# A two-layer streaming encoder on one core: another order of columns for TensorE's operands

## The chip, the core and the metric

The kernel runs on one core of one Trainium2 chip. The metric is the device time of one execution in microseconds (us), the median of repeated runs. One further execution was recorded by the hardware profiler; its trace is what the views below are taken from. The engines are called as the profile calls them: PE is TensorE's matmul, PEld its weight load, DVE is VectorE, ACT is ScalarE, POOL is GpSimd, SP is SyncE, which issues most of the DMAs.

## The reference

The reference is one inference step of a two-layer encoder with model width 2048. Layer 0 mixes frames by a gated MLP (gMLP), layer 1 by multi-scale retention with 8 heads; after each comes a dense SwiGLU layer with a hidden width of 5632, and after each of the four a LayerNorm of the residual sum. 256 frames of a new stream and 32 frames of a running one go through the same weights.

```python
def swiglu(x, w_in, w_out):
    gate, up = jnp.split(x @ w_in, 2, axis=-1)
    return (jax.nn.silu(gate) * up) @ w_out

def trunk(x, ...):
    for i in range(DEPTH):                       # 2
        if i % 2 == 0:
            h, v = gmlp_mix(x, w_a_in[j], ..., w_a_out[j])
        else:
            h, s = retention_mix(x, pos, states[j], w_b_in[j], w_b_out[j])
        x = layer_norm(ALPHA * x + h, ...)
        x = layer_norm(ALPHA * x + swiglu(x, w_ffn_in[i], w_ffn_out[i]), ...)
```

All data are float32. What costs the work are eight dense products: `a_in` (2048 to 4096), `a_out` (2048 to 2048), `b_in` (2048 to 12288), `b_out` (4096 to 2048), and for each of two layers `f_in` (2048 to 11264) and `f_out` (5632 to 2048), each for 288 frames.

## The kernel before

**Layout of the work.** Activations lie transposed: a channel of 128 in the partitions, the 288 frames (256 of the prompt, 32 of the running stream) along the free axis. Weights are the stationary operand in blocks of 128 x 128, the activations the moving operand with 288 columns, and an output tile of 128 channels x 288 frames gathers in one PSUM bank over all blocks of the contraction.

**Precision in three matmuls.** Each float32 value is split in a high part (rounded to the type fp32r) and a low part (what is left). `Core.step` therefore issues three fp32r matmuls for a block (lines 104 to 106): high weights by high activations, high weights by low activations, low weights by high activations. Every matmul of the program comes with its own weight load in the trace.

**Weights.** They come from HBM in the order of use, in chunks of 8 blocks: 128 partitions x 1024 values, 512 KB (`wpack`). `Core.prep` loads a chunk into one of three tiles `raw` (SP's queue, line 73) and splits it into `whi` (a copy on ACT, line 420) and `wlo` (a subtraction on DVE, line 421), of which there are four tiles each. It is called three chunks ahead. `Core.blk` (line 81) hands out block j of a chunk: in the kernel before, 128 adjacent columns. The order in which blocks are used is written down while the program is built, and the host packs `wpack` by it, outside the measured time.

**Order of the work.** The order on PE is the order of the program text. `Core.tiles` and `Core.group` run over output tiles; `evac` functions read a finished bank on ACT or DVE; `Core.after` puts small jobs (norms, transposes through DRAM, retention scores) a few output tiles later. The four accumulating banks rotate.

**Moving tiles.** `moving` (line 413) makes tiles whose rows are 320 values (1280 bytes) long and whose data begin 4 values (16 bytes) into a row. They hold the activations for `a_in`, `b_in`, `f_in` (`xh`, `xl`), `a_out` (`g_sh`, `g_sl`), `f_out` (`hh`, `hl`) and `b_out` (`r_oh`, `r_ol`). Just behind a LayerNorm the kernel starts the next product before the norm is known: `PostNorm.start` runs 12 output tiles with 290 columns, the 288 frames and two columns for gain and bias, and corrects the result afterwards. All other dense matmuls have 288 columns.

**Where the tiles lie.** Within a partition the program's layout puts 8,320 bytes of scratch and constants first, then eleven weight tiles of 4096 bytes (three `raw`, four `whi`, four `wlo`), which thus begin at 128 modulo 256, up to byte 53,376. Then comes the placeholder tile `shift` of line 900, 128 bytes that nothing uses, and `xh` at 53,504. All rows of moving tiles are multiples of 256 bytes apart, so the data of all of them begin at 16 modulo 256.

Of the kernel before, what the change touches and what calls it, by code (L numbers as in the profile page):

```python
# [10 lines left out]
F32 = mybir.dt.float32  # L11
# [8 lines left out]
P = 128  # L20
# [4 lines left out]
NT = NP + NS  # L25
# [13 lines left out]
CB = 8  # L39
# [7 lines left out]
class Core:  # L47
# [33 lines left out]
    def blk(self, w, k, m):  # L81
        i = len(self.order)
        self.order.append((w, k, m))
        c, j = divmod(i, CB)
        if j == 0:
            self.prep(c + 3)
            self.ready.pop(c - 1, None)
        hi, lo = self.ready[c]
        return hi[:, j * P:(j + 1) * P], lo[:, j * P:(j + 1) * P]

    def state(self, h):

# [6 lines left out]
    def step(self, ps, w, k, m, x, first, last):  # L99
        mm = self.nc.tensor.matmul  # L100
        hi, lo = self.blk(w, k, m)
        xh, xl = x
        n = xh.shape[-1]
        mm(ps[:, :n], hi, xh, start=first, stop=False)  # L104
        mm(ps[:, :n], hi, xl, start=False, stop=False)  # L105
        mm(ps[:, :n], lo, xh, start=False, stop=last)  # L106

    def accum(self, name):
        return self.acc.tile([P, 512], F32, tag="acc", name=name)
# [42 lines left out]
    def tiles(self, w, koff, ks, ms, x, evac, grouped=True, lag=2):  # L152

        nk = len(ks)
        if grouped:
            self.group(w, koff, ks, ms[:4], x, evac, lag=lag)
            ms = ms[4:]
        for m in ms:
            p = self.accum(f"a{w}_{m}_{self.ticks}")
            for i, k in enumerate(ks):  # L160
                self.step(p, w, koff + k, m, x(k), i == 0, i == nk - 1)
            evac(m, p)
            self.tick()


def rsqrt(nc, out, v, t):
# [246 lines left out]
def moving(pool, n, name, tag=None):  # L413

    t = pool.tile([P, n, ROW], F32R, name=name, **({"tag": tag} if tag else {}))
    return t[:, :, LEAD:]


def split(nc, hi, lo, f):
    nc.scalar.copy(hi, f)  # L420
    nc.vector.tensor_tensor(lo, f, hi.bitcast(F32), ALU.subtract)  # L421
# [140 lines left out]
def ffn(core, cst, x, y, lnp, layer, prev, out=None):  # L562
    tc, nc = core.tc, core.nc
    xh, xl = x
    xs = lambda k: (xh[:, k, :NT], xl[:, k, :NT])
    ln = PostNorm(core, cst, x, y, lnp, 2 * layer + 1, out)
    with tc.tile_pool(name=f"ffn{layer}", bufs=1, reuse_waits="tile") as pool:
        hh = moving(pool, HH, f"hh{layer}")
        hl = moving(pool, HH, f"hl{layer}")
        for half in range(2):  # L570
            sg = {}

            def evac(m, ps):
                if m < HT:
                    t = pool.tile([P, NT], F32, tag="sg", name=f"sg{layer}_{m}", bufs=4)
                    nc.scalar.activation(t, ps[:, :NT], AF.Silu)
                    sg[m] = t
                else:
                    j = m - HT
                    i = j - half * HH  # L580
                    f = pool.tile([P, NT], F32, tag="hf", name=f"hf{layer}_{j}", bufs=3)
                    nc.vector.tensor_tensor(f, ps[:, :NT], sg.pop(j), ALU.mult)
                    split(nc, hh[:, i, :NT], hl[:, i, :NT], f)

            ms = []
            for j in range(half * HH, (half + 1) * HH):
                ms += [j, HT + j]
            if half == 0:
                prev.start(f"f_in{layer}", ms, evac)
                ms = ms[4 * RAW:]  # L590
            core.tiles(f"f_in{layer}", 0, list(range(KT)), ms, xs, evac, grouped=False)
            core.tiles(f"f_out{layer}", half * HH, list(range(HH)), list(range(KT)),
                       lambda k: (hh[:, k, :NT], hl[:, k, :NT]),
                       ln.last if half else ln.part)
    return ln
# [297 lines left out]
@with_exitstack  # L893
def hybrid_step(ctx, tc, ins, outs):
    nc = tc.nc
    ctx.enter_context(tc.manual_schedule(engines={PE}))
    core = Core(ctx, tc, ins["wpack"])
    cp = ctx.enter_context(tc.tile_pool(name="cp", bufs=1))
    lnp = ctx.enter_context(tc.tile_pool(name="lnp", bufs=1))
    cp.tile([P, 32], F32, name="shift")  # L900
    lnp.tile([P, 32], F32, name="shift_lnp")
    xh = moving(cp, KT, "xh")
    xl = moving(cp, KT, "xl")
    y = cp.tile([P, KT, NT], F32, name="y")
    cst = {}
    cp.tile([P, 32], F32, name="shift_one")
    cst["one2048"] = cp.tile([P, P], F32, name="one2048")
    nc.gpsimd.memset(cst["one2048"], 1.0 / D)
    cst["ln"] = cp.tile([P, 4, 2, KT], F32, name="lnv")
    cst["one_r"] = cp.tile([P, P], F32R, name="one_r")  # L910
    nc.scalar.copy(cst["one_r"], cst["one2048"])
    warm = core.bank("warm")
    for _ in range(11):
        nc.tensor.matmul(warm[:, :P], cst["one2048"], cst["one2048"], start=True, stop=True)

    def load(k):
        if k < KT:
            if k % 2 == 0:
                nc.sync.dma_start(y[:, k:k + 2, :], ins["xT"][:, k:k + 2, :])
            split(nc, xh[:, k, :NT], xl[:, k, :NT], y[:, k, :])  # L920

    with tc.manual_schedule(engines={mybir.EngineType.DVE, mybir.EngineType.Activation}):
        core.prep(0, lambda: load(0))
        for k in range(1, 4):
            load(k)
            core.prep(k)
    x = (xh, xl)
    ln = gmlp(core, cst, x, y, lnp, ins, outs["v"], lambda s: load(s + 4))
    ln = ffn(core, cst, x, y, lnp, 0, ln)
    ln = retention(core, cst, x, y, lnp, ln, ins, outs["st_p"], outs["st_s"])  # L930
    ffn(core, cst, x, y, lnp, 1, ln, outs["yT"])
    core.flush()
    assert len(core.order) == NBLK + NSTATE
    return core.order
# [84 lines left out]
```

## Time and profile before

| what | value |
|---|---|
| median of 3 runs | 2854.0 us (2853.41 to 2855.37) |
| profiled execution: its time, its span from the first instruction to the last | 2852.41 us, 2850.6 us |
| PE busy | 2838.6 us, 100% of the span, 21574 matmuls |
| DVE, ACT, POOL busy | 1696.9, 1240.9, 141.8 us (60%, 44%, 5%) |
| granted TensorE clock | 0.999 |
| moved by DMA | 515.49 MB, 181 GB/s on the mean |

A matmul's time in the profile runs from its start until its last result is in PSUM, and matmuls overlap: the next one starts while the one before is still under way. What a matmul costs PE is therefore not its duration but the distance from its start to the next start, called its spacing here.

### The profile page before, as it was taken

What the parts mean: (1) busy time and instruction counts of PE and PEld (TensorE: products, weight loads), DVE (VectorE), ACT (ScalarE), POOL (GpSimd) and SP (SyncE); (2) the same over time, 40 slices, a digit from 0 to 9 for tenths busy, and PEclk for the clock granted to TensorE, in tenths of its full rate; (3) what the DMA queues carried; (4) which work ended last, traced back from release to release, by engine and by line L of the source; (5) the groups of instructions that cost most, each with busy time, mean ns of one, the idle gap of its engine ahead of it and who ended that gap; (6) DMA issues with size and microseconds to landing.
All of it is one profiled execution on the core that took longest, in us unless ns stands there. A gap on an engine that the chain in (4) does not pass through costs nothing.

```text
span 2850.6 us, 51421 instructions
## 1 busy us (share of the span) xinstructions
PE 2838.6 (100%) x21574; PEld 2823.6 (99%) x21574; DVE 1696.9 (60%) x2432; ACT 1240.9 (44%) x1642; POOL 141.8 (5%) x241
## 2 busy tenths in 40 slices
PE   9999999999999999999999999999999999999998
PEld 9999999999999999999999999999999999999998
DVE  5678864445444456777755566767854444444455
ACT  5544553333333344554443344444543333333343
POOL 1100000000000000012200111200000000000001
PEclk9999999999999999999999999999999999999999
DMA  8655555555555555566755566655555555555553
GB/s 280 214 174 163 164 170 169 168 168 169 170 170 170 170 172 171 179 203 226 227 190 170 190 214 210 221 189 169 164 169 170 170 168 168 169 169 170 170 168 124
DMA packets 146584, 515.49 MB, mean 181 GB/s; under 512 B 18016, under 2 KB 20336, under 8 KB 146320
## 3 DMA queue, kind: packets, MB, share of 16 engines
q1 hardware_dynamic: 131984, 473.47, 50.7%
q0 software_dynamic: 14224, 38.59, 4.3%
q8 instruction: 168, 2.75, 0.4%
q14 instruction: 64, 0.52, 0.1%
q10 hardware_dynamic: 144, 0.15, 0.0%
HBM read 486.98 MB, written 25.17 MB: 180 GB/s over the span
## 4 chain that ended last, share of the span: by engine, by line
PE 98%; DVE 1%; DMA 1%; issue 0%; ACT 0%; POOL 0%; SPq 0%; DVEq 0%; POOLq 0%
PE af_in L105 13%; PE af_in L104 13%; PE af_in L106 13%; PE ab_in L104 7%; PE ab_in L105 7%; PE ab_in L106 7%; PE af_out L106 6%; PE af_out L105 6%; PE af_out L104 6%; PE aa_in L105 2%; PE aa_in L106 2%; PE ab_out L105 2%; PE ab_out L104 2%; PE ab_out L106 2%; PE aa_in L104 2%; PE aa_out L105 1%
## 5 line engine op out<-in xcount | busy, mean ns | idle before, releaser
L421 DVE TENSOR_TENSOR wlo<-raw,whi 128x1024 fp32r<-128x1024 f32 (+1 forms) x892 | 1085.6, 1219 | 917.8 <-ACT whi L420 913.6
L420 ACT CAST whi<-raw 128x1024 fp32r<-128x1024 f32 (+1 forms) x892 | 931.9, 1046 | 1452.5 <-PE af_in L105 343.9
L105 PE MATMUL af_in<-xl,whi 128*128 128x288 f32 (+1 forms) x2816 | 824.7, 293 | 0.0
L106 PE MATMUL af_in<-xh,wlo 128*128 128x288 f32 (+1 forms) x2816 | 824.7, 293 | 0.0
L104 PE MATMUL af_in<-xh,whi 128*128 128x288 f32 (+1 forms) x2816 | 824.6, 293 | 0.0
L104 PEld LDWEIGHTS af_in<-xh,whi 128*128 128x128 f32 x2816 | 528.6, 188 | 0.0
L106 PEld LDWEIGHTS af_in<-xh,wlo 128*128 128x128 f32 x2816 | 528.6, 188 | 0.0
L105 PEld LDWEIGHTS af_in<-xl,whi 128*128 128x128 f32 x2816 | 528.6, 188 | 0.0
L104 PE MATMUL ab_in<-xh,whi 128*128 128x288 f32 (+1 forms) x1536 | 450.6, 293 | 0.0
L105 PE MATMUL ab_in<-xl,whi 128*128 128x288 f32 (+1 forms) x1536 | 450.1, 293 | 0.2
L106 PE MATMUL ab_in<-xh,wlo 128*128 128x288 f32 (+1 forms) x1536 | 449.9, 293 | 0.0
L104 PE MATMUL af_out<-hh,whi 128*128 128x288 f32 x1408 | 411.8, 292 | 0.0
L105 PE MATMUL af_out<-hl,whi 128*128 128x288 f32 x1408 | 411.8, 292 | 0.0
L106 PE MATMUL af_out<-hh,wlo 128*128 128x288 f32 x1408 | 411.8, 292 | 0.0
L105 PEld LDWEIGHTS ab_in<-xl,whi 128*128 128x128 f32 x1536 | 288.4, 188 | 1.8 <-DVE xl L421 0.7
L104 PEld LDWEIGHTS ab_in<-xh,whi 128*128 128x128 f32 x1536 | 288.4, 188 | 1.1
L106 PEld LDWEIGHTS ab_in<-xh,wlo 128*128 128x128 f32 x1536 | 288.4, 188 | 0.0
L104 PEld LDWEIGHTS af_out<-hh,whi 128*128 128x128 f32 x1408 | 264.3, 188 | 0.0
L105 PEld LDWEIGHTS af_out<-hl,whi 128*128 128x128 f32 x1408 | 264.3, 188 | 0.0
L106 PEld LDWEIGHTS af_out<-hh,wlo 128*128 128x128 f32 x1408 | 264.3, 188 | 0.0
L104 PE MATMUL aa_in<-xh,whi 128*128 128x288 f32 x512 | 150.4, 294 | 0.0
L105 PE MATMUL aa_in<-xl,whi 128*128 128x288 f32 x512 | 149.9, 293 | 0.1
(249 smaller groups left out, 2920.5 us busy)
## 6 DMA issues: line engine op xcount, KB each, us to landing
raw<-in_wpack_dram SPq DMA_DIRECT2D x887, 512.0 KB, 3.4
v_room<-tv POOLq DMA_DIRECT2D x32, 144.0 KB, 4.5
of<-o_room POOLq DMA_DIRECT2D x32, 144.0 KB, 4.2
vw<-v_room POOLq DMA_DIRECT2D x8, 512.0 KB, 6.2
out_st_s_dram<-sso POOLq DMA_DIRECT2D x16, 256.0 KB, 2.8
o_room<-to POOLq DMA_DIRECT2D x8, 512.0 KB, 3.7
out_st_p_dram<-so POOLq DMA_DIRECT2D x16, 256.0 KB, 5.9
y<-in_xT_dram SPq DMA_DIRECT2D x8, 288.0 KB, 4.6
```

Source lines behind the costliest of these rows:

```text
L104: mm(ps[:, :n], hi, xh, start=first, stop=False)
L105: mm(ps[:, :n], hi, xl, start=False, stop=False)
L106: mm(ps[:, :n], lo, xh, start=False, stop=last)
L420: nc.scalar.copy(hi, f)
L421: nc.vector.tensor_tensor(lo, f, hi.bitcast(F32), ALU.subtract)
```

## The change

There are three edits, made together.

1. The 8 blocks of a chunk lie in 4 pairs. Within a pair the columns alternate: column 0 of the first block, column 0 of the second, column 1 of the first, and so on. The host packs them so, and `blk` hands out every second column of a pair (a step of 8 bytes). The chunks that hold a retention state, not weights, stay as they were.
2. A matmul with 288 moving columns takes them in another order. `turned` regards the columns as 72 groups of four (16 bytes); first come the groups 0, 3, 6, ..., 69, then 1, 4, ..., 70, then 2, 5, ..., 71. The moving operand and the PSUM output are addressed in the same order, so every result lands where it did. Matmuls with 290 columns keep the plain order.
3. The placeholder `shift` has 64 values in place of 32. All that is laid out behind it moves by 128 bytes; the weight tiles, which lie ahead of it, stay. By the layout above the data of moving tiles then begin at 144 modulo 256 (the words that go with the change say 160).

```diff
@@ blk
-        return hi[:, j * P:(j + 1) * P], lo[:, j * P:(j + 1) * P]
+        return tuple(t[:, j // 2 * 2 * P + j % 2:(j // 2 + 1) * 2 * P:2] for t in (hi, lo))
@@ step
-        n = xh.shape[-1]
-        mm(ps[:, :n], hi, xh, start=first, stop=False)
-        mm(ps[:, :n], hi, xl, start=False, stop=False)
-        mm(ps[:, :n], lo, xh, start=False, stop=last)
+        ps = ps[:, :xh.shape[-1]]
+        if xh.shape[-1] == NT:
+            ps, xh, xl = turned(ps), turned(xh), turned(xl)
+        mm(ps, hi, xh, start=first, stop=False)
+        mm(ps, hi, xl, start=False, stop=False)
+        mm(ps, lo, xh, start=False, stop=last)
@@ new function
+def turned(v):
+    return v.rearrange("p (g a c) -> p a g c", a=3, c=4)
@@ hybrid_step
-    cp.tile([P, 32], F32, name="shift")
+    cp.tile([P, 64], F32, name="shift")
@@ kernel (on the host)
-            wpack[c, :, j * P:(j + 1) * P] = mats[w][k * P:(k + 1) * P, m * P:(m + 1) * P]
+            pairs = wpack[c].reshape(P, CB // 2, P, 2)
+            pairs[:, j // 2, :, j % 2] = mats[w][k * P:(k + 1) * P, m * P:(m + 1) * P]
```

## The prediction

> **What bounds the kernel now.** I read the page first: its busy times, then the chain that ended last.
>
> ```profile
> span 2850.6 us, 51421 instructions
> PE 2838.6 (100%) x21574; PEld 2823.6 (99%) x21574; DVE 1696.9 (60%) x2432; ACT 1240.9 (44%) x1642; POOL 141.8 (5%) x241
> PEclk9999999999999999999999999999999999999999
> PE 98%; DVE 1%; DMA 1%; issue 0%; ACT 0%; POOL 0%; SPq 0%; DVEq 0%; POOLq 0%
> ```
>
> PE is never without work, at full clock, and it is 98% of the chain. So the time is the sum of the spacings of its matmuls. How many there are is in the view of groups with shapes kept apart; line 104 stands here for lines 105 and 106 too, which have the same counts.
>
> ```profile
> L104 PE MATMUL af_out<-hh,whi 128*128 128x288 f32 x1408 | 411.8, 292 | 0.0
> L104 PE MATMUL af_in<-xh,whi 128*128 128x288 f32 x2432 | 711.4, 292 | 0.0
> L104 PE MATMUL ab_in<-xh,whi 128*128 128x288 f32 x1344 | 393.9, 293 | 0.0
> L104 PE MATMUL aa_in<-xh,whi 128*128 128x288 f32 x512 | 150.4, 294 | 0.0
> L104 PE MATMUL ab_out<-r_oh,whi 128*128 128x288 f32 x512 | 149.8, 292 | 0.0
> L104 PE MATMUL aa_out<-g_sh,whi 128*128 128x288 f32 x256 | 75.1, 293 | 0.0
> L104 PE MATMUL af_in<-xh,whi 128*128 128x290 f32 x384 | 113.3, 295 | 0.0
> L104 PE MATMUL ab_in<-xh,whi 128*128 128x290 f32 x192 | 56.6, 295 | 0.0
> ```
>
> That is 3 x 6464 = 19,392 matmuls of 288 columns and 3 x 576 = 1,728 of 290. Their spacing comes from the timeline of PE, first for 288 columns, then for 290 (first and last of a run).
>
> ```profile
> 1000.12 0.29 PE L104 MATMUL af_in<-xh,whi 128*128 128x288 f32 x1
> ...
> 1002.07 0.29 PE L104 MATMUL af_in<-xh,whi 128*128 128x288 f32 x1
> ```
>
> ```profile
> 316.12 0.29 PE L105 MATMUL af_in<-xl,whi 128*128 128x290 f32 x1
> ...
> 318.92 0.29 PE L105 MATMUL af_in<-xl,whi 128*128 128x290 f32 x1
> ```
>
> The first pair spans 15 matmuls: 1.95 / 15 = 130 ns. The second spans 21: 2.80 / 21 = 133.3 ns. So 288 columns take 19,392 x 0.130 = 2521 us and 290 columns 1,728 x 0.1333 = 230 us, together 2751 of the span's 2850.6; the other 99 us are the small matmuls, the first loads and the last norm, which the change hardly touches. One nanosecond of spacing on the 288-column matmuls is worth 19.4 us, 0.7%.
>
> **Is 130 ns the least that 288 columns can take?** Two views say no. The plain fp32 matmuls at the end have the same 288 columns; each matmul of the program is two instructions there.
>
> ```profile
> 2836.91 0.65 PE L343 MATMUL off<-y,centring 128*128 128x288 f32 x2
> 2837.39 0.65 PE L344 MATMUL off<-b,centring 128*128 128x288 f32 x2
> 2837.88 0.65 PE L343 MATMUL off<-y,centring 128*128 128x288 f32 x2
> 2838.36 0.65 PE L344 MATMUL off<-b,centring 128*128 128x288 f32 x2
> 2838.85 0.65 PE L343 MATMUL off<-y,centring 128*128 128x288 f32 x2
> ```
>
> From 2836.91 to 2838.85 there are 8 instructions, 242 ns each. If each streams its columns twice (the even multiple says so; no row proves it), one stream is 121 ns. There a weight load falls on every second stream only. The second view is that of the tiles `wlo` and `one_r`, with minimum, median and maximum durations.
>
> ```profile
> L106 PE MATMUL ab_in<-xh,wlo x1536: 289/293/303, 1140.1 to 1907.5; 128*128 128x288 f32 x168, 128*128 128x290 f32 x24
> L287 PE MATMUL m<-s,one_r x16: 289/294/299, 320.0 to 2834.3; 128*128 128x288 f32 x16
> L106 PE MATMUL af_out<-hh,wlo x1408: 292/292/293, 590.9 to 2833.8; 128*128 128x288 f32 x176
> ```
>
> In steady state a duration of 292 to 293 goes with a spacing of 130. After an odd-sized matmul, when PE's weight load and its stream begin in another relation to each other, the same shape shows 289 to 303: spacings from 126.5 to about 140. So part of the 130 is a meeting of two reads that depends on their relation, and this is what all three edits alter.
>
> [...]
>
> **The change part by part.** Host packing is outside the time; chunks stay 512 KB and contiguous, so DMA, ACT and DVE do the same instructions on the same bytes. PE issues the same instructions with other addresses. No wait is added.
>
> *Pairs.* A load now takes 128 columns from 64 groups of 16 bytes (the four values that the change keeps together), formerly from 32. The trace shows no strided load; the nearest rows are contiguous loads of 128 and 64 columns:
>
> ```profile
> L104 PEld LDWEIGHTS af_in<-xh,whi x2816: 187/188/192, 313.5 to 2696.0; 128*128 128x128 f32 x188
> L784 PEld LDWEIGHTS os<-whi,qi x16: 134/136/137, 1250.9 to 1864.2; 128*64 128x64 f32 x16
> ```
>
> 64 columns cost 188 - 136 = 52 ns, 0.81 ns each, so the loading proper takes 104 of the 130 ns and hides beside the stream. If the price goes by column, nothing changes. If it goes by group, 104 becomes 208, and loads set the spacing: (208 - 130) x 21,120 = 1647 us more. I take the first: the moving stream draws 72 groups in 130 ns, 1.8 ns each, from the same memory, and 64 groups at that rate are 116 ns, which still fits under 121.
>
> *Turned columns.* The stream reads whole groups, 48 bytes apart, and writes PSUM in the same order. The best is the 121 ns of a stream that meets nothing: a gain of 9 ns. The worst that I can price is one column's time (130 / 288 = 0.45 ns) at each of 71 jumps, 32 ns: 162 ns.
>
> *Shift.* Moving data go from 16 to 144 modulo 256 while weights stay at 128: another relation, bounded by the 126.5 to 140 above, either way.
>
> The three act on one spacing and can't be added; together it lies between 121 and 162 ns. I take 124, the middle between 121 (nothing met) and 126.5 (the best that contiguous reads have shown), because each edit alters exactly the relation on which 126.5 to 140 depends: stepping by two, a load crosses 1024 bytes in its 104 ns rather than 512, about the pace of a plain stream (1152 in 130), and the turn makes the stream cross three times as many.
>
> *The 290-column matmuls* get the pairs and the shift but not the turn. Bounds 126.5 to 140: -12 to +12 us; I take 0. A gain there would partly come back as a wait, because the chain leaves PE in that stage for a transfer that doesn't get faster:
>
> ```profile
> 1197.91 1.88 POOL v_room L429 x3
> 1199.79 4.92 DMA v_room<-tv
> 1204.75 1.56 issue
> 1206.33 6.11 DMA vw<-v_room
> 1212.45 1.06 ACT vv L420
> ```
>
> *What is late next.* The cover of a faster PE is the engine that splits weights. Its fullest stage, 250 to 400 us in the view by windows:
>
> ```profile
> 250.00:400.00 150.00, 150.00 (x1141) 150.00 (x1140) 128.44 (x222) 86.78 (x138) 0.58 (x1) 1.00 0.51 163
> raw<-in_wpack_dram SPq DMA_DIRECT2D x887, 512.0 KB, 3.4
> ```
>
> DVE is 128.4 / 150 = 86% busy there; at 124 / 130 of the time it is 90%. A chunk of 24 matmuls lasts 2.98 us in place of 3.12, and a load of 3.4 us has three tiles to land in. Neither binds.
>
> **Sum.** Against the profiled execution (2852.4 us, span 2850.6): 19,392 x 6 ns = 116 us, so 2736. The median of the runs shown is 1.6 us above that execution: **2738 us**, 4.1% faster.
>
> **The rivals.**
>
> *Little of it goes.* Only the phase improves, by 1 to 2.5 ns: 128 ns gives 2854 - 39 = 2815. For it: 512-column matmuls, whose weight load covers less than half of the stream, lose as much in proportion, so part of the stall may be the stream's own:
>
> ```profile
> 1267.23 2.80 PE sp L863 x12
> ```
>
> 2.80 / 12 = 233 ns for 512 columns is 0.456 ns a column, against 0.451 at 288. Against it: the turn alters the stream's own order as well.
>
> *Nothing changes.* The 9 ns are a rate of fp32r streaming, whatever the addresses: 2854. For it: six different moving tiles all show 292 to 294. Against it: 289 to 303.
>
> *The bad phase holds (slower).* Place: every dense matmul. The relation after the shift is the one that now occurs after odd-sized matmuls, and twice as many groups per load make it meet each time. Price: 303 - 293 = 10 ns on 288 columns and 6.7 on 290: 194 + 12 = 206 us, 3060 us. It decides from any steady spacing above 130. Against it: in the trace a long spacing is followed by a short one, so the stall is not held.
>
> *Broken runs in PSUM or SBUF cost (slower).* 162 ns: 32 x 19,392 = 621 us, 3475 us. For it: two more columns, half a group, cost 133.3 - 130 = 3.3 ns rather than 0.9. Against it: here all groups are whole.
>
> [...]
>
> **How the numbers follow.** Forecast (121 to 127 ns) 0.60, little of it 0.14, nothing 0.08, bad phase 0.10, broken runs or loads by group 0.08. Faster by over 0.2% (about what a measurement of this kernel can tell from no change): 0.60 + 0.14 = 0.74; within: 0.08; slower: 0.18. The lowest time is 121 ns on 288 columns and 122 on 290: 175 + 20 us less, 2659, which all must go right for; I put the low end at 2668. Upward it takes in little and nothing, to 2860; the slower cases, 0.18, are left out, and 0.02 below. The forecast's own range is 2668 to 2796 (127 ns).
>
> **What would show it.** Right: 15 matmuls of 288 columns in about 1.86 us, durations near 286, 290 columns still at 133, PE still 100% busy with fewer us, loads at 188. Loads near 290 show pricing by group. Spacing above 130 refutes the forecast; spacing unchanged after all three edits shows that addresses don't matter. PE gaps with DVE as the releaser would show that the split of weights has become the bound.

## The result, and the profile after

The changed kernel takes 2834.5 us (median of 4 runs, 2832.4 to 2837.0) against 2854.0 us of the kernel before: a ratio of 0.9931, with a 95% interval of 0.9914 to 0.9949. It is faster, by 19.5 us and not by the 116 us of the forecast.

The page of the changed kernel: span, busy times, granted clock and the chain that ended last.

```profile
span 2831.8 us, 51419 instructions
PE 2818.8 (100%) x21574; PEld 2804.0 (99%) x21574; DVE 1696.5 (60%) x2432; ACT 1241.5 (44%) x1642; POOL 141.4 (5%) x241
PEclk9999999999999999999999999999999999999999
PE 98%; DVE 1%; DMA 1%; ACT 0%; issue 0%; POOL 0%; SPq 0%; DVEq 0%; POOLq 0%; ACTq 0%
```

The picture is the same: PE is the chain, at full clock, with the same 21,574 matmuls; DVE and ACT do the same work. Only the spacing moved. A short way to read it, used for every kernel below, is a view by windows of PE's row: stretch, length, busy us with the matmuls that touch the stretch, clock, DMA. The first stretch lies in a stage of 290-column matmuls, the other two in stages of 288 columns (`f_in` and `f_out` of layer 0). A duration of 292 ns is 2.2 spacings of 130, so two matmuls are under way when a stretch begins, and the spacing is its length over the count less two. Before and after:

```profile
325.00:385.00 60.00, 60.00 (x452) 1.00 0.50 160
940.00:1020.00 80.00, 80.00 (x617) 1.00 0.56 179
1040.00:1120.00 80.00, 80.00 (x618) 1.00 0.52 172
```

```profile
325.00:385.00 60.00, 60.00 (x447) 1.00 0.49 160
940.00:1020.00 80.00, 80.00 (x623) 1.00 0.54 177
1040.00:1120.00 80.00, 80.00 (x623) 1.00 0.51 172
```

Before, 80 / 615 is 130.1 ns; after, 80 / 621 is 128.8 ns. At 290 columns, 60 / 450 = 133.3 ns became 60 / 445 = 134.8 ns. Over all spacings of the two traces the means are 130.0 and 128.9 ns for 288 columns, 133.4 and 134.4 ns for 290. That accounts for the time: 19,392 x -1.1 = -21 us, 1,728 x 1.0 = +2 us, together -19 of a span that fell by 18.8. The loads got longer too (`wlo` as a tile, durations minimum, median, maximum; lines 104 to 106 are 106 to 108 now):

```profile
L108 PEld LDWEIGHTS af_out<-hh,wlo x1408: 192/195/196, 588.9 to 2814.7; 128*128 128x128 f32 x176
L108 PE MATMUL af_out<-hh,wlo x1408: 289/291/295, 589.1 to 2814.9; 128*128 128x288 f32 x176
```

195 ns stood at 188 before, and the steady stage of `f_out`, where every matmul took 292 or 293, now mixes 289 to 295.

### The profile page after: what moved, and what is told of

Read it like the earlier page. It is cut to its first block, busy times and chain, and to the rows that moved or that the text cites. A ratio compares the mean times of both kernels' runs of the same rounds, so it can differ in the third digit from the quotient of the medians.

```text
span 2831.8 us, 51419 instructions
## 1 busy us (share of the span) xinstructions
PE 2818.8 (100%) x21574; PEld 2804.0 (99%) x21574; DVE 1696.5 (60%) x2432; ACT 1241.5 (44%) x1642; POOL 141.4 (5%) x241
## 4 chain that ended last, share of the span: by engine, by line
PE 98%; DVE 1%; DMA 1%; ACT 0%; issue 0%; POOL 0%; SPq 0%; DVEq 0%; POOLq 0%; ACTq 0%
PE af_in L108 13%; PE af_in L107 13%; PE af_in L106 13%; PE ab_in L106 7%; PE ab_in L108 7%; PE ab_in L107 7%; PE af_out L107 6%; PE af_out L108 6%; PE af_out L106 6%; PE ab_out L108 2%; PE ab_out L106 2%; PE ab_out L107 2%; PE aa_in L108 2%; PE aa_in L107 2%; PE aa_in L106 2%; PE aa_out L108 1%
## 5 line engine op out<-in xcount | busy, mean ns | idle before, releaser
L108 PEld LDWEIGHTS af_in<-xh,wlo 128*128 128x128 f32 x2816 | 550.5, 196 | 0.0
L107 PEld LDWEIGHTS af_in<-xl,whi 128*128 128x128 f32 x2816 | 545.8, 194 | 0.0
L106 PEld LDWEIGHTS af_in<-xh,whi 128*128 128x128 f32 x2816 | 544.1, 193 | 0.0
L106 PEld LDWEIGHTS ab_in<-xh,whi 128*128 128x128 f32 x1536 | 299.7, 195 | 1.1
L108 PEld LDWEIGHTS ab_in<-xh,wlo 128*128 128x128 f32 x1536 | 297.8, 194 | 0.0
L107 PEld LDWEIGHTS ab_in<-xl,whi 128*128 128x128 f32 x1536 | 296.8, 193 | 0.9
L108 PEld LDWEIGHTS af_out<-hh,wlo 128*128 128x128 f32 x1408 | 273.9, 195 | 0.0
L107 PEld LDWEIGHTS af_out<-hl,whi 128*128 128x128 f32 x1408 | 273.4, 194 | 0.0
L106 PEld LDWEIGHTS af_out<-hh,whi 128*128 128x128 f32 x1408 | 271.8, 193 | 0.0
L108 PE MATMUL aa_in<-xh,wlo 128*128 128x288 f32 x512 | 149.4, 292 | 1.1 <-DVE wlo L428 1.1
```

Of the source, the lines that this page charges most:

```text
L106: mm(ps, hi, xh, start=first, stop=False)
L107: mm(ps, hi, xl, start=False, stop=False)
L108: mm(ps, lo, xh, start=False, stop=last)
```

## The experiments

The theory after the result (A) was that of the prediction, a load and a stream that meet, with the changed kernel at an unlucky address; its rival (B) that the stream alone is slow, by its own order, and that only the turn matters.

### Many small series in one trace

A spacing can be measured by itself. Behind the last output of the kernel before I put 86 short series of matmuls, each with its own start address, order of weight columns and order of moving columns. The weights of the series begin at 128 modulo 256, as those of the kernel do.

```diff
+        for i, (o, w, x, out, n, cols, reps) in enumerate(plan):
+            dst = order(ps[:cols, :n], out)
+            for r in range(reps):
+                for j in range(CB):
...
+                    nc.tensor.matmul(dst, weights(wh, j, w, cols), xh, start=r == 0 and j == 0, stop=False)
+                    nc.tensor.matmul(dst, weights(wh, j, w, cols), xl, start=False, stop=False)
+                    nc.tensor.matmul(dst, weights(wl, j, w, cols), xh, start=False, stop=r == reps - 1 and j == CB - 1)
```

> The kernel before with 86 short series of matmuls added behind its last output (48 to 192 matmuls of a series, in the high-high, high-low, low-high order of the dense step, on constant data, results unread; the kernel's own work is unchanged, so its time is longer by the series). Each series has one start address of the moving data (0, 16, ..., 240 modulo 256, weights at 128), weights as adjacent or every second column, moving columns plain or as every third group of four; others load fewer weight columns, take other column counts or other orders. Theory A (a load and a stream meet in the memory): spacing at 16 modulo 256, plain, adjacent weights is 130 as in the kernel; it changes by several ns over the 16 start addresses; a load of 64 columns brings it to 125 or less, 512 columns cost less per column than 288. Theory B (the stream itself is slow at this rate): all start addresses and both weight orders show 130 with plain columns; 64-column loads still 130; only the order of the moving columns changes it.

Four series in the timeline of PE, first and last matmul of 48 each (47 spacings): adjacent weights with plain columns at 16 modulo 256 (`qac`); adjacent, turned, at 128 (`qaz`); pairs, turned, at 144 (`qcg`) and at 160 (`qch`).

```profile
2877.85 0.29 PE L937 MATMUL qac__31013<-mb_h,mb_wh 128*128 128x288 f32 x1
...
2883.96 0.29 PE L939 MATMUL qac__31013<-mb_h,mb_wl 128*128 128x288 f32 x1
...
3023.27 0.29 PE L937 MATMUL qaz__32140<-mb_h,mb_wh 128*128 128x288 f32 x1
...
3029.22 0.29 PE L939 MATMUL qaz__32140<-mb_h,mb_wl 128*128 128x288 f32 x1
...
3230.90 0.29 PE L937 MATMUL qcg__33757<-mb_h,mb_wh 128*128 128x288 f32 x1
...
3236.96 0.29 PE L939 MATMUL qcg__33757<-mb_h,mb_wl 128*128 128x288 f32 x1
3237.09 0.29 PE L937 MATMUL qch__33806<-mb_h,mb_wh 128*128 128x288 f32 x1
...
3243.05 0.29 PE L939 MATMUL qch__33806<-mb_h,mb_wl 128*128 128x288 f32 x1
```

6.11 / 47 = 130.0 ns is the kernel before, 6.06 / 47 = 128.9 ns the changed kernel, each met by a series with its address and orders while no other engine was at work on the core. 5.95 / 47 = 126.6 is what the turned order reaches at 128 with weights as they were. The spacings in ns over the 16 start addresses, with five of them. Each is the mean of a series without its first six spacings, which still settle; values of series given below without a division are taken in the same way.

| weights, columns | least to most | 16 | 128 | 144 | 160 | 240 |
|---|---|---|---|---|---|---|
| adjacent, plain (before: 16) | 130.0 to 134.6 | 130.0 | 131.7 | 131.8 | 133.3 | 134.6 |
| adjacent, turned | 126.7 to 133.3 | 130.0 | 126.7 | 130.1 | 131.6 | 126.7 |
| pairs, plain | 131.2 to 133.4 | 133.4 | 133.4 | 133.4 | 132.1 | 133.2 |
| pairs, turned (after: 144) | 126.7 to 132.2 | 130.0 | 131.2 | 128.9 | 126.7 | 131.2 |

The kernel before already stood at the best address that plain columns have. The changed one stands at a middling one for its orders; 160, the address in the words that go with the change, is 16 bytes further. Neither theory holds whole. B falls, since address and weight order matter. A falls in its price: a load of 64 columns at 16 gave 129.3 ns, not 125, one of 32 columns 130.0, and 512 columns took 233.3 ns, which is 0.456 a column and not less than the 0.451 of 288. At that address, with plain columns, the length of the load hardly matters, as B had it.

### One edit at a time

The three edits each alone, on the kernel before: `blk` and the packing; the two lines in `step`; the placeholder.

```diff
+        return tuple(t[:, j // 2 * 2 * P + j % 2:(j // 2 + 1) * 2 * P:2] for t in (hi, lo))
```

> Only the weights lie in pairs; plain moving columns, old start address. Theory A: the load crosses twice the bytes, so the meeting changes: spacing other than 130, between 126.5 and 140, load durations 190 to 196 as in the changed kernel; time 2785 to 3050 us. Theory B: 130 and 2854 us within 0.2%; the load durations may grow, hidden.

```diff
+        if xh.shape[-1] == NT:
+            ps, xh, xl = turned(ps), turned(xh), turned(xl)
```

> Only the moving columns are turned; adjacent weights, old start address. Theory A: spacing changes, but not to the 128.9 of the changed kernel, which needs all three: 130 or more. Theory B: the whole gain is here: 128.9 at 288 columns, 2834 us; 290 columns still 133.3.

```diff
-    cp.tile([P, 32], F32, name="shift")
+    cp.tile([P, 64], F32, name="shift")
```

> Only the moving tiles begin 128 bytes later; plain columns, adjacent weights. Theory A: the relation of load and stream is another: spacing between 126.5 and 140 but not 130.0 for 288 and not 133.3 for 290 columns; time 2785 to 3060 us. Theory B: 130 and 133.3, 2854 us within 0.2%.

Pairs alone: 2920.2 us, ratio 1.0232 (1.0215 to 1.0249). Turn alone: 2854.0 us, 1.0001 (0.9991 to 1.0010). Shift alone: 2884.7 us, 1.0108 (1.0093 to 1.0123). Two of the windows of each, in this order:

```profile
325.00:385.00 60.00, 60.00 (x445) 1.00 0.49 163
940.00:1020.00 80.00, 80.00 (x602) 1.00 0.49 166
```

```profile
325.00:385.00 60.00, 60.00 (x452) 1.00 0.49 165
940.00:1020.00 80.00, 80.00 (x618) 1.00 0.53 175
```

```profile
325.00:385.00 60.00, 60.00 (x452) 1.00 0.50 167
940.00:1020.00 80.00, 80.00 (x610) 1.00 0.52 173
```

80 / 600 = 133.3 ns, 80 / 616 = 129.9 and 80 / 608 = 131.6, as the series have them at 16, 16 and 144. The shift alone leaves the mean of 290 columns at 60 / 450 = 133.3 ns, which A had not expected. None of the edits helps alone, and two of them hurt. So B is out, and the gain of the three together is no sum of gains.

### Each edit left out

Without the shift:

```diff
-    cp.tile([P, 64], F32, name="shift")
+    cp.tile([P, 32], F32, name="shift")
```

> The changed kernel without the shift: pairs and turned columns, moving data at 16 modulo 256. Theory C: 130.0 at 288 columns as in the series, and 290 columns with pairs 135.6 in place of 133.3, so 2854 + 4 = 2858 us within 5 us. Rival (pairs and turn bring the gain wherever the data begin): 128.9 and 2834 us.

Without the pairs (turned columns, adjacent weights, 144; the packing on the host goes back with it):

```diff
-        return tuple(t[:, j // 2 * 2 * P + j % 2:(j // 2 + 1) * 2 * P:2] for t in (hi, lo))
+        return hi[:, j * P:(j + 1) * P], lo[:, j * P:(j + 1) * P]
```

> The changed kernel without the pairs: turned columns, moving data at 144 modulo 256, adjacent weights. Theory of relation (start address, order of loads, order of stream decide together): 130.05 as in the series, 290 columns 133.3 as with the shift alone: 2854 us within 6. Rival (pairs only cost): below 2834.

Without the turn (pairs, plain columns, 144):

```diff
-        if xh.shape[-1] == NT:
-            ps, xh, xl = turned(ps), turned(xh), turned(xl)
```

> The changed kernel without the turn: pairs, moving data at 144 modulo 256, plain columns. Theory of relation: 133.4 as in the series, 2854 + 66 = 2920 us within 8. Rival (pairs and shift carry the gain): 2834.

Without the turn it is 2917.3 us, 1.0219 (1.0204 to 1.0234), as expected. The other two missed: 2821.2 us without the shift, 0.9887 (0.9871 to 0.9904), and 2819.2 us without the pairs, 0.9876 (0.9858 to 0.9893). Both are faster than the changed kernel and than their series. The rival of the second, that pairs only cost, asked for less than 2834 us and has its number.

With these runs all eight combinations of the three edits are measured (us):

| columns | adjacent, 16 | pairs, 16 | adjacent, 144 | pairs, 144 |
|---|---|---|---|---|
| plain | 2854.0 | 2920.2 | 2884.7 | 2917.3 |
| turned | 2854.0 | 2821.2 | 2819.2 | 2834.5 |

The turn gains between 0 and 99 us and costs in no column. The pairs cost 66 and 33 us with plain columns and 15 us with turned columns at 144, but gain 33 us with turned columns at 16, so it is not true everywhere that they only cost. The shift gains 35 us beside the turn alone, costs 31 us by itself and 13 us beside both others, and makes no clear difference beside the pairs alone (3 us).

The windows of the kernel without the pairs show how a kernel comes to be faster than its series:

```profile
940.00:1020.00 80.00, 80.00 (x634) 1.00 0.55 180
1040.00:1120.00 80.00, 80.00 (x617) 1.00 0.55 180
```

The same orders at the same address run at 80 / 632 = 126.6 ns in one stage and at 80 / 615 = 130.1 in the next. The mean over 24 matmuls at a time is 127 from 395 us to 1031 and 130 from there on, until the next stage of 290 columns. What lies at the border is in PE's timeline: one matmul of the LayerNorm, with other weights and another tile.

```profile
1030.32 0.29 PE L108 MATMUL af_out<-hh,wlo 128*128 128x288 f32 x1
1030.45 0.29 PE L267 MATMUL cen<-cen,one_r 128*128 128x288 f32 x1
1030.58 0.29 PE L106 MATMUL af_out<-hh,whi 128*128 128x288 f32 x1
```

The kernel without the shift shows the same, 80 / 632 and then 80 / 616:

```profile
940.00:1020.00 80.00, 80.00 (x634) 1.00 0.54 179
1040.00:1120.00 80.00, 80.00 (x618) 1.00 0.53 178
```

So two steady spacings, 126.6 and 130.1 ns, exist at one address, and in these two kernels a stage keeps the one that it has fallen into. In layer 1 the same border stands at the same place, at 2706 us without the pairs and 2708 us without the shift. In both kernels and both layers the 126.7 begins with the first 288-column matmul behind the 290-column matmuls of `f_in`; behind those of `b_in` it doesn't. That the `cen` matmul throws the spacing over is read from the place of the borders; moving that matmul was not tried.

### The address that the words name, and a better one

The changed kernel with `LEAD` 8, so that moving data begin at 160:

```diff
-LEAD = 4
+LEAD = 8
```

> The changed kernel with its moving data 16 bytes further in each row (LEAD 8 in place of 4), so that they do begin at 160 modulo 256. Theory C (start address and the two orders alone set the spacing, as in the series of the run with series): 126.7 in place of 128.9 at 288 columns, 2834.5 - 2.2 x 19.4 = 2792 us, within 8 us for the 290-column matmuls. Theory D (what the changed kernel has above 126.7 comes from the other engines' work beside it): no better than 2834 within 6 us.

2837.5 us, 0.9943 (0.9928 to 0.9957): no gain on the changed kernel. Theory C, the address and the orders alone, missed. The number is that of theory D, work of the other engines, but such work is no general reason: the next kernel and the last reach 126.7 ns beside the same work. The windows:

```profile
325.00:385.00 60.00, 60.00 (x431) 1.00 0.49 159
940.00:1020.00 80.00, 80.00 (x626) 1.00 0.54 179
1040.00:1120.00 80.00, 80.00 (x626) 1.00 0.51 170
```

Here 288 columns run at 80 / 624 = 128.2 ns (126.7 in `a_out`, 130.0 in much of `b_in`; the mean of all is 128.5), and the 290-column matmuls at 60 / 429 = 139.9. With pairs the first series had 290 columns at address 16 only; a later one at 160 gives 139.4. That costs 1,728 x 5.5 = 9.5 us against the changed kernel and eats the 0.4 x 19.4 = 8 us of the others. In `b_out` a border at a `cen` matmul goes the other way: 130.0 ns on the mean of the stretch before it, 126.7 behind it (from 1930 us on).

Turned columns with adjacent weights, at 128:

```diff
-LEAD = 4
+LEAD = 0
...
-        return tuple(t[:, j // 2 * 2 * P + j % 2:(j // 2 + 1) * 2 * P:2] for t in (hi, lo))
+        return hi[:, j * P:(j + 1) * P], lo[:, j * P:(j + 1) * P]
```

> Turned moving columns, weights in adjacent columns as before the change, moving data at 128 modulo 256 (LEAD 0 behind the larger placeholder). Theory C: 126.7, so 2854 - 3.3 x 19.4 = 2790 us, within 10 us for the 290-column matmuls. Rival (the gain needs the pairs): 130 and 2854 us, or more.

2794.4 us, 0.9789 (0.9775 to 0.9804), as expected, with the same spacing on both sides of `cen`:

```profile
325.00:385.00 60.00, 60.00 (x452) 1.00 0.49 160
940.00:1020.00 80.00, 80.00 (x634) 1.00 0.55 179
1040.00:1120.00 80.00, 80.00 (x634) 1.00 0.58 189
```

The pairs are not needed. The turn is, by the series (131.7 ns with plain columns at 128), and so is an address at which the short spacing holds.

### Load and stream, apart and moved against each other

Other series behind the kernel before: loads of 32 columns, and the weights moved while the moving data stay.

```diff
+                    nc.tensor.matmul(dst, weights(wh[:, wo:], j, w, cols), xh, start=r == 0 and j == 0, stop=False)
```

> The kernel before with 90 other series behind its last output (constant data, results unread, the kernel's own work unchanged): loads of 32 columns at all 16 start addresses, plain and turned; the weights' start moved in steps of 16 bytes while the moving data stay; 290 columns at all 16 start addresses; turned 240, 264, 300, 312 columns. Theory M (load and stream meet): moving the weights by d bytes gives what moving the data by -d gave before (turned, pairs, data at 144: 126.7 for weights moved by 240, 130.0 for 128); with 32-column loads the 16 addresses differ less than the 131 to 134.6 and 126.7 to 133.3 of full loads. Theory S (the stream alone, by its own address): moving the weights changes nothing (128.9 and 130.0 throughout), and 32-column loads show the same 16 values as full loads.

First and last of three series: 32-column loads at 144 with plain (`qak`) and at 128 with turned columns (`qaz`); and full loads in pairs, turned, data at 144, weights moved by 176 bytes (`qbr`).

```profile
2928.35 0.29 PE L937 MATMUL qak__31405<-mb_h,mb_wh 128*32 128x288 f32 x1
...
2934.59 0.30 PE L939 MATMUL qak__31405<-mb_h,mb_wl 128*32 128x288 f32 x1
...
3020.85 0.29 PE L937 MATMUL qaz__32140<-mb_h,mb_wh 128*32 128x288 f32 x1
...
3026.81 0.29 PE L939 MATMUL qaz__32140<-mb_h,mb_wl 128*32 128x288 f32 x1
...
3132.26 0.29 PE L937 MATMUL qbr__33022<-mb_h,mb_wh 128*128 128x288 f32 x1
...
3138.21 0.29 PE L939 MATMUL qbr__33022<-mb_h,mb_wl 128*128 128x288 f32 x1
```

With 32-column loads the turned stream takes 126.7 ns at 15 of 16 addresses (130.0 at the other), here 5.96 / 47; the plain stream still takes 128.9 to 133.1, here 6.24 / 47 = 132.8, a spread of 4.2 ns beside 4.6 with full loads. So with plain columns most of the spread is the stream's own; the turn all but frees the stream from its address, and what is left of the stall under turned columns (126.7 to 133.3 ns with full loads) comes with the load. Weights moved by 176 give 5.95 / 47 = 126.6, as data moved by -176 to 224 did. Of the two moves named beforehand, 240 gave its 126.7 and 128 missed (126.7, not 130.0). Of the 15 such moves, 9 agree within 0.8 ns for pairs and turned columns, 11 for adjacent and plain; the others differ by 0.9 to 4 ns. Theory S is out, and M holds in the main: the relation decides, though not it alone.

### Is there anything below 126.7?

89 series with other orders, and with only one side turned.

```diff
+            dst = order(ps[:cols, :n], out)
+                    xh, xl = order(mh[:, row], x), order(ml[:, row], x)
```

> The kernel before with 89 other series behind its last output (constant data, results unread, the kernel's own work unchanged): many orders of the moving columns (every a-th group of c columns), at 128 modulo 256, with loads of 32 and of 128 adjacent columns; and only the reads or only the PSUM writes turned. Theory F (126.7 is the least that a stream of 288 columns takes): no order is below 126.6, also with 32-column loads. Rival (121, as the plain fp32 streams of the prediction): some order comes to 121 to 125. For the PSUM side: if its order costs or brings nothing, only the reads turned gives 126.7 and only the writes turned gives what plain gives at 128, about 131.7.

Adjacent weights at 128, only the reads turned (`qdi`) and only the PSUM writes turned (`qdj`):

```profile
3415.16 0.29 PE L937 MATMUL qdi__35129<-mb_h,mb_wh 128*128 128x288 f32 x1
...
3421.14 0.29 PE L939 MATMUL qdi__35129<-mb_h,mb_wl 128*128 128x288 f32 x1
3421.26 0.29 PE L937 MATMUL qdj__35178<-mb_h,mb_wh 128*128 128x288 f32 x1
...
3427.45 0.30 PE L939 MATMUL qdj__35178<-mb_h,mb_wl 128*128 128x288 f32 x1
```

Here 5.98 / 47 is 127.2, because the first spacings of `qdi` reach 138; without the first six it is 126.7, and `qdj` is 131.6. Plain on both sides gives 131.6 too. At this address the order of the reads does all, that of the writes nothing. No order of 288 columns is below 126.6, with full or with short loads, which supports theory F as far as these orders go.

### The fastest

Turned columns and adjacent weights (`blk` and the packing as in the kernel at 128) at 240, where a series had 290 plain columns at 131.3 ns:

```diff
-LEAD = 4
+LEAD = 28
```

> Turned moving columns, adjacent weights, moving data at 240 modulo 256 (LEAD 28 behind the larger placeholder). By the series: 126.7 at 288 columns (as at 128), and 131.3 at 290 columns in place of 133.6 at 128: 2794 - 2.3 x 1.73 = 2790 us within 5. Rival (several steady spacings are possible at one address, and the kernel falls into a longer one): 288 columns above 127.5, 2805 us or more.

2791.0 us, 0.9780 (0.9763 to 0.9796), as expected:

```profile
325.00:385.00 60.00, 60.00 (x460) 1.00 0.51 168
940.00:1020.00 80.00, 80.00 (x634) 1.00 0.54 179
1040.00:1120.00 80.00, 80.00 (x633) 1.00 0.57 185
```

60 / 458 = 131.0 ns for 290 columns, 126.6 and 126.8 for 288. This beats both kernels: the turn is the only one of the three edits in it that is not an address.

## Why the prediction was right and wrong

What failed is the size of the main term. It was 19,392 x 6 ns = 116 us; measured are 1.1 ns (130.0 to 128.9), 21 us. Three steps led to it: the floor, the choice of 124, and the pairs.

**Right: what bounds the time, and the sign.** The spacing of the matmuls is the time, one nanosecond is 19.4 us, and the change acts there alone. Nothing became late behind it; the split of weights keeps up even at 126.7 ns, where PE is idle for 16 us of the span (data at 128) against 12 before. The sign was partly luck: of the 16 addresses with pairs and turned columns, 7 have series clearly below 130.0 (under 129.5) and 6 clearly above it (over 130.5). The first view behind the claim that two reads meet, durations of 289 to 303 for one shape, led the right way: with the data at 144, weights moved by 176 bytes bring 126.6 ns in place of 128.9. What the two reads share was not shown.

**Wrong: the floor of 121 ns.** I took it from the plain fp32 matmuls, whose instructions take 242 ns each; that each of them streams its columns twice, with a load for every second stream only, was my estimate, and no run shows it (the rows have one load for each instruction). No series of 288 fp32r columns is below 126.6, not even turned and with a load of a quarter. Of the 9 ns that I counted as stall only 3.3 were had by any kernel or series here.

**Wrong: the choice of 124 within the bounds.** For the shift I set bounds in both directions and then took the middle of the two good ends, as if a new relation could only be a better one. The addresses spread over 126.7 to 132.2 ns for pairs and turned columns; the changed kernel drew 128.9. The argument names no address without a table of them, and the trace before has one address only; its rows bore a value between 126.5 and 130, not below. The rival "little of it goes", given 0.14, is what came in size, near the lower edge of its 1 to 2.5 ns.

**Wrong: the pairs at nothing.** Loads take 7 ns more (188 to 195), neither the 0 of pricing by column nor the 104 of pricing by group. Alone they cost 3.3 ns of spacing, 66 us. Leaving them out of the changed kernel gains 15 us, while adding them to the turn alone gains 33 us. So they have no price of their own, and that a load at the stream's pace would help was an argument without a row, which these runs do not bear out.

**Right in size: 290 columns near 0** (+2 us within -12 to +12), though at 160 with pairs their spacing reaches 139.9, at the upper bound.

**The slower rivals.** Broken runs in PSUM cost nothing for groups of four (at 128, with plain reads, 131.6 ns with the writes turned and with the writes plain). The bad phase exists, and two of the edits alone bring one that lasts: 133.3 and 131.6 ns in steady state. My argument against it, that a long spacing is followed by a short one, was read from a single relation.

**Open.** Why one address has several steady spacings, and what makes 128 and 240 good, is not settled. Which of them a stage takes can't be told from the series; three of the kernels (without the shift, without the pairs, at 160) differed from theirs by 1.8 ns on the mean. The series themselves are not free of it: ten of them were run in two traces, nine agree within 0.1 ns, and one (adjacent weights, every fourth group of four, 16) gave 130.0 and 126.6.

## What to carry to other kernels

Where PE is the chain, measure its spacing and not its duration, and find the floor with short series of the same type of matmul in one trace, not from another type. A start address is worth trying in steps of 16 bytes together with the order of columns (126.7 to 134.6 ns here), for every shape that the kernel uses, and an edit must be tried with and without its companions: here the turn never cost, while the pairs and the shift helped or hurt depending on the other two. A steady spacing should then be checked in every stage, since here it changed at a single odd matmul, from 126.6 to 130.1 ns.

## What was not expected of the hardware

- One shape, one address and one order can have two steady spacings, 126.7 and 130.0 ns, each lasting for a hundred us and more. Many steady means lie at 126.7, 130.0 or 133.3 ns; others lie between (128.9 in the changed kernel, 131.6 with the shift alone).
- The least seen for 288 fp32r columns is 126.7 ns, while each of the two instructions of a plain fp32 matmul of 288 columns takes 242.
- Groups of two columns (every third group), read and written so, double the spacing, 12.51 / 47 = 266 ns; with every fourth weight column loaded, a load lasts 330 ns in place of 188 and the spacing is 11.04 / 47 = 235 ns, so the load may be the bound there, which no run tested. Both lie in the first run with series:

```profile
3339.87 0.47 PE L937 MATMUL qcx__34590<-mb_h,mb_wh 128*128 128x288 f32 x1
...
3350.91 0.40 PE L939 MATMUL qcx__34590<-mb_h,mb_wl 128*128 128x288 f32 x1
...
3389.66 0.43 PE L937 MATMUL qdd__34884<-mb_h,mb_wh 128*128 128x288 f32 x1
...
3402.17 0.45 PE L939 MATMUL qdd__34884<-mb_h,mb_wl 128*128 128x288 f32 x1
```

  Every second column, two values out of 16 bytes, costs a load only 7 ns (195 in the changed kernel). For columns in groups of two the reads and the writes were not tried apart, so which of them doubles the time is open.
